# Delta heads' inverse from blocks of 16 instead of 8, half of the odd layer's lower halves on GpSimd, and odd-layer constants issued later

## The chip, the cores and the metric

The kernel runs on one core of a Trainium2 chip. The metric is the device time of one execution in microseconds (us). Three runs of the kernel before took 2287.2, 2292.83 and 2294.88 us, with a median of 2292.83. Engines are named as the profile names them: PE is the matrix engine (TensorE; PEld are its weight loads), DVE the vector engine, ACT the scalar engine, POOL is GpSimd, and SP is the queue that issues the DMA transfers.

## The reference

It is one inference step of two layers for a prompt of 1024 tokens and for 8 single samples, with the same weights; all data are fp32. Each layer normalizes x, projects it with one large matrix, runs its heads, gates them, and projects back:

```python
h = _rms(x, norm_w[layer]) * (1.0 + scale) + shift
# even layer: 8 gated-delta heads (A) and 8 mLSTM heads (B)
# odd layer:  4 GLA heads (C) and 4 retention heads (D)
y = jnp.concatenate([o_first, o_second], axis=-1) * jax.nn.silu(z)
x = x + gate * (y @ w_out)
```

A gated-delta head solves a unit lower triangular system in every chunk of tokens:

```python
kk = jnp.einsum('bthd,bshd->bhts', kc, kc)
A = jnp.where(tri_strict, decay * kk, 0.0) * beta_h[..., :, None]
U = lax.linalg.triangular_solve(A + eye, rhs, left_side=True, lower=True, unit_diagonal=True)
```

The outputs are the normalized x of prompt and samples and the new states of all heads.

## The kernel before

Prompt and samples stand side by side as 1032 columns (W), with the 1024 channels of x in 8 tiles of 128 partitions. Projections are computed in fp32 exactness from two halves: `load_w` (L889) loads a weight tile of 1024 rows by 128 columns in eight pieces (`wf`), and `halves` (L896) makes its rounded copy `whi` on ACT and the rest `wlo = wf - whi` on DVE. There are two buffers of each. Every projection then takes three matmuls per piece: whi with the high half of h, whi with the low half, and wlo with the high half. The columns are worked in three parts of 344 (NB), so a weight tile feeds 8 x 3 x 3 = 72 matmuls into three PSUM banks (`pj`).

All operations are recorded first (`Recorder`, L181) and not issued in the order of the code. A planner gives each a cost (`_cost` for DVE, ACT, POOL and SP; `_pe_cost`, L139, for PE), then places them on the five engines by readiness and priority (`forward`, L367), with priorities from a backward pass (`backward`, L310), several times over; the order with the shortest planned time is emitted. So each engine has a fixed order of instructions that depends on all the costs. An entry in `after` makes later recorded operations wait for a given one. As a consequence, nearly every row of the profile has one source line, L451, and rows are told apart by their tiles.

Gated-delta heads use chunks of 128 tokens, 8 chunks per head. `inverse` (L1293) gets the strictly lower triangular N of all chunks and forms the inverse of (I + N) by blocks. First, the 32x32 diagonal blocks (four per chunk) go to DRAM (`nd`), are read back so that each 8x8 diagonal block lies on a partition of its own (128 partitions), and DVE inverts these blocks by substitution, one column per step: 7 steps of two instructions. The result goes through DRAM again (`yd`) into the tile D (slot `EM`), 32 rows of four diagonal blocks side by side. Then the block size is doubled: 8 to 16 and 16 to 32 in the loop `for i in range(1, 3)`, each round with 32 matmuls of 32x32 (N times D), a masked copy on DVE, another 32 matmuls, a subtract and a 32x32 transpose on DVE; then 32 to 64 and 64 to 128 with larger matmuls. The identity that the substitution starts from is copied on POOL from the constant `i8`; the mask of each round is read out of the constant `icode`.

At the end of a layer, `out_proj` (L1947) reads the 16 tiles of y back from DRAM (`yd`) and splits each into halves (`split`). The tiles 14 and 15, which come last, are split late. `odd_setup` (L1660) loads the odd layer's constants: masks and decay tables (`lmask`, `rdm`, `rin`, `rend`), the low-rank weights (`gla_w2`), and the rotary tables. In the odd layer, POOL makes the products of the GLA heads (`s_tmp<-s_EM`), several of the rounding sums, and the `pow` of the norm.

Of the kernel before, what the change touches and what calls it, by code (L numbers as in the profile page):

```python
# [9 lines left out]
F32 = mybir.dt.float32  # L10
F32R = mybir.dt.float32r
AF = mybir.ActivationFunctionType
ALU = mybir.AluOpType
# [11 lines left out]
NC = T // L  # L25
# [14 lines left out]
def host_constants():  # L40
    f = np.float32
    c = {}
    c["ident"] = np.eye(128, dtype=f)
    pos = np.concatenate([np.arange(T), np.full(NS, 8192)]).astype(f)
    inv = (f(10000.0) ** (-np.arange(64, dtype=f) / f(64))).astype(f)
    ang = (pos[None, :] * inv[:, None]).astype(f).astype(np.float64)
    c["cosT"] = np.concatenate([np.cos(ang), np.cos(ang)], 0).astype(f)
    c["sinT"] = np.concatenate([np.sin(ang), -np.sin(ang)], 0).astype(f)
    lg = np.log(1.0 - 2.0 ** (-5.0 - np.arange(4)))
    s, t = np.arange(L)[:, None], np.arange(L)[None, :]  # L50
    dm = np.zeros((L, 4, L))
# [12 lines left out]

    code = np.zeros((32, 32), f)
    for i in range(2):
        code[lm[:, 1 - i, :].T > 0] = 1.0 + i
    c["icode"] = np.tile(code, (4, 1))
    c["i8"] = np.tile(np.eye(8, dtype=f).reshape(1, 64), (128, 1))

    sel = np.zeros((2, 4, 8, 4, 32), f)
    for to, at in enumerate((1, 0, 2, 3)):
        for i in range(8):
            sel[:, at, i, to, i] = 1.0
    c["sel"] = sel.reshape(64, 128)
    return c
# [62 lines left out]
def _pe_cost(method, out, args, kw):  # L139

    if method == "transpose":
        return (109.0 if args[1].shape[0] > 64 else 60.0), "whole"
    n, rows, cols = _elems(kw["rhs"]), kw["lhsT"].shape[0], kw["lhsT"].shape[1]
    if kw["rhs"].dtype == F32R:
        return 0.45 * n + 2.5, "pass"
    if kw.get("tile_position") is not None and cols <= 32:
        return (max(1.87 * n / 4, 15.0) if rows > 32 else 15.0), (rows, cols)
    if rows <= 64 and cols <= 64:
        return max(1.67 * n + 9, 117.0), (rows, cols)
    kind = "whole" if rows == 128 and (cols == 128 or kw.get("tile_position") is None) else (rows, cols)  # L150
    return 2 * max(0.833 * n + 2.5, 111.0) + 90 * (n == 130), kind
# [315 lines left out]
class Step:  # L467
# [428 lines left out]
    def halves(self, w, n=KT):  # L896
        hi, lo = (self.wtile(x, [128, KT, 128])[:, 0:n] for x in ("whi", "wlo"))
        self.act(hi, w[:, 0:n], AF.Copy)
        self.nc.vector.tensor_tensor(lo, w[:, 0:n], hi, op=ALU.subtract)
        return hi, lo  # L900

    def proj_parts(self, parts, ks):
# [390 lines left out]
    def inverse(self, N):  # L1293

        V, G, dma = self.nc.vector, self.nc.gpsimd, self.nc.sync.dma_start

        nd, yd = (self.nyd[x][self.turn(x, 2)] for x in ("nd", "yd"))
        by32 = lambda x, j: x.rearrange("(c j q) x -> c j (q x)", c=NC, j=4)[:, j, 0:1024].rearrange(
            "c (s t) -> s c t", t=32)
        by8 = lambda x: x[:, 0:256].rearrange("m (r t) -> m r t", t=32)[:, :, 0:8]  # L1300
        blocks = [slice(32 * j, 32 * j + 32) for j in range(4)]
        for j, b in enumerate(blocks):
            dma(by32(nd, j), N[b, :, b])
        n8, y8, t8 = (self.const([128, 8, 8], x) for x in ("n8", "y8", "t8"))
        dma(n8, by8(nd))
        G.tensor_copy(y8, self.i8)
        for s in range(7):
            n = 7 - s
            V.tensor_tensor(t8[:, 0:s + 1, 0:n], y8[:, 0:s + 1, s:s + 1].to_broadcast([128, s + 1, n]),
                            n8[:, s:s + 1, s + 1:8].to_broadcast([128, s + 1, n]), op=ALU.mult)  # L1310
            V.tensor_tensor(y8[:, 0:s + 1, s + 1:8], y8[:, 0:s + 1, s + 1:8], t8[:, 0:s + 1, 0:n], op=ALU.subtract)
        dma(by8(yd), y8)

        t = self.slot("EM", name="inv")
        D, At, qt, Dt = (t[:, 256 * i:256 * i + 256].rearrange("p (c t) -> p c t", c=NC) for i in range(4))
        for j, b in enumerate(blocks):
            dma(D[b], by32(yd, j))
        V.transpose(Dt, D)
        for i in range(1, 3):
            p = self.ps(None, [128, NC, 32])  # L1320
            for c in range(NC):
                for j, b in enumerate(blocks):
                    self.mm(p[b, c, :], N[b, c, b], Dt[b, c, :], tile_position=(32 * j, 32 * j))
            V.scalar_tensor_tensor(At, self.icode.unsqueeze(1).to_broadcast([128, NC, 32]), float(i), p,
                                   op0=ALU.is_equal, op1=ALU.mult)
            p = self.ps(None, [128, NC, 32])
            for c in range(NC):
                for j, b in enumerate(blocks):
                    self.mm(p[b, c, :], At[b, c, :], D[b, c, :], tile_position=(32 * j, 32 * j))
            V.tensor_tensor(D, D, p, op=ALU.subtract)  # L1330
            V.transpose(Dt, D)
        Y = self.slot("Y", [128, NC, L], name="Y")
        G.memset(Y, 0.0)
        for b in blocks:
# [12 lines left out]
        for c in range(NC):  # L1347
            for i in (0, 2):
                j = i + 1
# [271 lines left out]
    def even_setup(self):  # L1621
        nc, a, V, G = self.nc, self.a, self.nc.vector, self.nc.gpsimd
        self.bkq = self.const([128, 258], "bkq")
        G.memset(self.bkq, 0.0)
        self.icode = self.const([128, 16], "icode").bitcast(mybir.dt.bfloat16)
        self.i8 = self.c_load("i8", [128, 8, 8])
        zero = self.slot("aT", [128, 264], name="zero")
        G.memset(zero, 0.0)
        for x in self.nyd["yd"]:
            self.nc.sync.dma_start(x, zero)  # L1630
        code = self.slot("EM", [128, 32], name="code")
        self.nc.sync.dma_start(code, self.a["icode"])
        self.nc.vector.tensor_copy(self.icode, code)
        self.vs = self.const([128, 2, NS], "mvs")
        self.ozs = self.const([128, 2, NS], "mozs")
        self.nms = self.const([128, 2, 2, NS], "mnms")
        self.mC = self.const([128, 4, 130], "C")
        for x in range(2):
            G.memset(self.mC[64 - 64 * x:128 - 64 * x, 2 * x:2 * x + 2, :], 0.0)
        self.qq = self.const([128, 2, 2, NS], "mqq")  # L1640
        G.memset(self.qq, 0.0)

        nt = self.slot("q2", [32, 128], name="snt")
        nc.sync.dma_start(nt, a["state_mlstm_n"][0].rearrange("b (q x) d -> (b q) (x d)", x=2))
        p = self.ps()
# [13 lines left out]

    def odd_setup(self):  # L1660
        nc, a = self.nc, self.a
        self.lmask = self.c_load("lmask", [128, 6, 32])
        self.rdm = self.c_load("rdm", [128, 4, L])
        self.rin = self.c_load("rin", [128, 4, L])
# [5 lines left out]
        nc.sync.dma_start(self.cosT, a["cosT"])  # L1670
        self.sinT = self.slot("mk", name="sinT")
        nc.sync.dma_start(self.sinT, a["sinT"])
        self.glr = self.slot("va", name="glr")
        self.qk_w = [self.load_w(a["od_w_in"][0], c) for c in (0, 512)]

# [271 lines left out]
    def out_proj(self, src, l, mod):  # L1947
# [45 lines left out]
        def x_in(n):  # L1993
            x = xs[n % 2] if last else self.x_slot(n)
            nc.sync.dma_start(x, self.xd[l][n])
            return x
# [57 lines left out]
            G.tensor_tensor(wl[:, 1], w, wl[:, 0], op=ALU.subtract)  # L2054
        for k in late:
            split(k)
        x2 = [x_in(n) for n in range(2)]
        for n in range(2):
            for j in range(3):
# [61 lines left out]
    def build(self):  # L2121
        tc, nc = self.tc, self.nc
        with ExitStack() as ctx:
# [20 lines left out]
            self.sd = [dr.tile([16, 128], F32, name=f"sd{i}") for i in range(2)]  # L2144
            self.spd = dr.tile([16, W], F32, name="spd")
            self.rd = [dr.tile([4, QB], F32, name=f"rd{i}") for i in range(2)]
            self.nyd = {x: [dr.tile([128, 264], F32, name=f"{x}{i}") for i in range(2)] for x in ("nd", "yd")}
            self.program()
            with tc.manual_schedule():
                self.nc.emit()  # L2150
# [103 lines left out]
```

## Time and profile before

| | |
|---|---|
| Runs | 2287.2, 2292.83, 2294.88 us; median 2292.83 |
| Profiled execution | 2289.05 us, span 2287.0 us |
| PE busy | 2221.4 us (97%), 18844 instructions |
| DVE busy | 1382.8 us (60%), 2700 instructions |
| ACT busy | 747.7 us (33%), 1374 instructions |
| POOL busy | 527.7 us (23%), 385 instructions |
| Mean granted PE clock | 0.987 |

The first number of an engine is the time in which it had an instruction running, and the share is that of the span. The heads of the even layer lie from about 100 to 1175 us (the delta heads' inverses from 188 to 1085), the even layer's output projection from there to about 1360, and the odd layer from there to the end, with its output projection from about 2090 on. The place where the even layer's heads end and its output projection begins (1157 to 1180) is called the layer boundary. An fp32 matmul with fp32 operands is recorded twice, so a block of 32 small matmuls shows as 64 instructions. A matmul's duration is longer than its distance to the next one, since matmuls overlap; what it costs is read from the starts.

### The profile page before, as it was taken

The page shows a single profiled execution, that of the slowest core. Times are in us where ns is not written, and L with a number is a line of the kernel's source. Part 1 is how long each engine was busy: PE and PEld are TensorE (multiplying, and loading weights), DVE is VectorE, ACT ScalarE, POOL GpSimd, SP SyncE. Part 2 cuts the span into 40 slices and gives each one's busy share as a digit, 9 for nine tenths or more (in the row PEclk, how much of TensorE's full clock was granted, in tenths as well). Part 3 has the DMA queues.
Part 4 walks back from the last instruction along what each step waited for, and adds up shares of the span by engine and source line. Part 5 has one row for each costly group of instructions (what it writes and reads, how often), then busy time and mean ns, then how long its engine had stood idle before and what let it go on. Part 6 is the DMA issues. An engine that isn't in the chain of part 4 may idle for free.

```text
span 2287.0 us, 44726 instructions
## 1 busy us (share of the span) xinstructions
PE 2221.4 (97%) x18844; PEld 2070.0 (91%) x18844; DVE 1382.8 (60%) x2700; ACT 747.7 (33%) x1374; POOL 527.7 (23%) x385
## 2 busy tenths in 40 slices
PE   6999999999999999999989999999999999998998
PEld 5777788899999999899989999999999999997997
DVE  6774646565564646556453355876976876977332
ACT  4422323232233233232331134234225324334322
POOL 3121112111123012211330031422422422433100
PEclk8999999999999999999999999999999999998999
DMA  9362544422143212432362221233142143246222
GB/s 260 124 165 60 152 133 121 129 77 72 40 118 105 69 52 86 108 95 72 114 216 84 75 76 38 56 122 107 43 136 94 50 133 95 56 149 209 74 58 91
DMA packets 285455, 235.20 MB, mean 103 GB/s; under 512 B 47819, under 2 KB 257733, under 8 KB 285246
## 3 DMA queue, kind: packets, MB, share of 16 engines
q1 hardware_dynamic: 285254, 232.35, 34.6%
q8 instruction: 147, 2.41, 0.4%
q14 instruction: 54, 0.44, 0.1%
HBM read 185.59 MB, written 46.91 MB: 102 GB/s over the span
## 4 chain that ended last, share of the span: by engine, by line
PE 88%; DMA 4%; DVE 4%; issue 1%; ACT 1%; POOL 1%; SPq 1%; POOLq 0%; DVEq 0%; ACTq 0%
PE pj L451 68%; PE A L451 14%; PE B L451 6%; DMA wf<-in_ev_w_in 1%; SPq L451 1%; DMA s_aT<-rd 0%; DVE s_h L451 0%; DMA s_h<-in_x_prompt 0%; DVE arena L451 0%; DVE s_N L451 0%; DMA s_pt<-yd 0%; DVE s_pt L451 0%; DMA ed<-s_Y 0%; DMA s_mp<-gd 0%; DVE s_mp L451 0%
## 5 line engine op out<-in xcount | busy, mean ns | idle before, releaser
L451 PE MATMUL pj<-s_h,whi 128*128 128x344 f32 (+1 forms) x6024 | 1498.6, 327 | 10.8 <-ACT s_h L451 5.4
L451 PEld LDWEIGHTS pj<-s_h,whi 128*128 128x128 f32 (+1 forms) x6024 | 1042.7, 189 | 44.8 <-issue 25.3
L451 PE MATMUL pj<-s_h,wlo 128*128 128x344 f32 (+1 forms) x3024 | 982.2, 325 | 1.5 <-DVE wlo L451 0.9
L451 PEld LDWEIGHTS pj<-s_h,wlo 128*128 128x128 f32 (+1 forms) x3024 | 569.8, 189 | 16.1 <-issue 10.6
L451 DVE TENSOR_TENSOR wlo<-wf,whi 128x1024 fp32r<-128x1024 f32 (+1 forms) x144 | 192.9, 1340 | 291.2 <-ACT whi L451 272.3
L451 ACT ACTIVATE whi<-wf 128x1024 fp32r<-128x1024 f32 (+2 forms) x146 | 152.1, 1043 | 374.9 <-PE pj L451 330.3
L451 ACT ACTIVATE s_pt<-pj 128x344 f32<-128x344 f32 (+1 forms) x170 | 77.0, 453 | 288.3 <-PE pj L451 282.8
L451 POOL TENSOR_TENSOR arena<-arena,base 128x8 f32<-128x8 f32 (+5 forms) x38 | 64.4, 1697 | 377.8 <-DVE arena L451 377.1
L451 POOL TENSOR_TENSOR s_tmp<-s_EM 128x512 f32<-128x512 f32 (+1 forms) x60 | 88.5, 1493 | 156.2 <-PE A L451 69.1
L451 DVE SCALAR_TENSOR_TENSOR s_pt<-s_u,base,s_pt 128x1024 f32<-128x1024 f32 x72 | 96.5, 1341 | 0.3
L451 ACT ACTIVATE s_u<-pj 128x344 f32<-128x344 f32 x93 | 41.9, 453 | 142.4 <-PE pj L451 80.2
L451 DVE SCALAR_TENSOR_TENSOR arena<-arena,A 128x128 f32<-128x128 f32 (+1 forms) x84 | 32.8, 391 | 84.5 <-PE A L451 83.9
L451 DVE STREAM_TRANSPOSE s_kd<-s_u 32x256 f32<-32x256 f32 x128 | 55.8, 436 | 16.6 <-ACT s_u L451 13.5
L451 POOL TENSOR_TENSOR s_tmp<-s_tmp,arena 128x1024 f32<-128x1024 f32 (+2 forms) x26 | 43.4, 1676 | 88.6 <-PE A L451 62.2
L451 POOL TENSOR_TENSOR s_kd<-s_kd,s_vs 128x1032 f32<-128x1032 f32 x8 | 21.5, 2688 | 167.6 <-ACT s_vs L451 152.2
L451 DVE SCALAR_TENSOR_TENSOR s_zz<-s_pt,pj 128x344 f32<-128x344 f32 x96 | 48.4, 507 | 18.7 <-ACT s_pt L451 17.9
L451 DVE STREAM_TRANSPOSE s_vs<-s_v 32x256 f32<-32x256 f32 x128 | 55.8, 436 | 1.9
L451 ACT ACTIVATE arena<-A,arena 128x128 f32<-128x128 f32 x64 | 23.5, 368 | 100.8 <-PE A L451 100.5
L451 ACT ACTIVATE s_tmp<-s_tmp 128x1024 f32<-128x1024 f32 (+1 forms) x44 | 46.1, 1054 | 28.7 <-POOL s_tmp L451 24.0
L451 DVE SCALAR_TENSOR_TENSOR arena<-arena,B 64x130 f32<-64x130 f32 (+1 forms) x84 | 31.2, 371 | 38.6 <-PE B L451 37.2
L451 ACT ACT_TABLE_LOAD x41 | 52.6, 1283 | 5.2 <-DMA s_h<-in_x_prompt 4.5
L451 POOL MEMSET s_u<- 128x3 f32 x24 | 2.4, 101 | 208.5 <-DVE s_pt L451 208.5
(643 smaller groups left out, 3597.7 us busy)
## 6 DMA issues: line engine op xcount, KB each, us to landing
wf<-in_ev_w_in SPq DMA_DIRECT2D x64, 512.0 KB
wf<-in_od_w_in SPq DMA_DIRECT2D x48, 512.0 KB
wf<-in_ada_w SPq DMA_DIRECT2D x32, 512.0 KB
s_pt<-yd SPq DMA_DIRECT2D x24, 516.0 KB
s_tmp<-sd SPq DMA_DIRECT2D x24, 512.0 KB
yd<-s_qg SPq DMA_DIRECT2D x15, 516.0 KB
wf<-in_ev_w_out SPq DMA_DIRECT2D x14, 512.0 KB
wf<-in_od_w_out SPq DMA_DIRECT2D x14, 512.0 KB
```

The costliest lines, as they stand in the source:

```text
L451: op.fn(*[self.placed(x) for x in op.args], **{k: self.placed(x) for k, x in op.kw.items()})
```

## The change

It has four parts.

1. `inverse` starts from blocks of 16: 64 partitions hold one 16x16 block each, the substitution takes 15 steps of two DVE instructions, and one doubling (16 to 32) is left in front of the larger ones. The identity is loaded by DMA into the working tile, and the mask is a plain product with `imask`. `even_setup` loads imask and no longer builds icode and i8.
2. `_pe_cost` gives tiles of at most 32 columns a higher cost: 25.6 instead of 15 ns for 32 columns of data and more than 32 rows, and 18 instead of 15 ns for 32 rows or fewer.
3. `halves` puts every second subtract of the odd layer on POOL.
4. The loads of `odd_setup` up to the rotary tables are recorded with `after` set to the last split of out_proj.

```diff
     if kw.get("tile_position") is not None and cols <= 32:
-        return (max(1.87 * n / 4, 15.0) if rows > 32 else 15.0), (rows, cols)
+        return (max(0.8 * n, 20.0) if rows > 32 else 18.0), (rows, cols)
...
         self.act(hi, w[:, 0:n], AF.Copy)
-        self.nc.vector.tensor_tensor(lo, w[:, 0:n], hi, op=ALU.subtract)
+        (self.nc.gpsimd if self.layer == "odd" and self.turn("half", 2) else self.nc.vector).tensor_tensor(lo, w[:, 0:n], hi, op=ALU.subtract)
...
+        t = self.slot("EM", name="inv")
+        D, At, qt, Dt = (t[:, 256 * i:256 * i + 256].rearrange("p (c t) -> p c t", c=NC) for i in range(4))
+        nb, yb, tb = (t[0:64, 256 * i:256 * i + 256].rearrange("p (r t) -> p r t", t=16) for i in (1, 2, 3))
+        dma(yb, self.a["i16"].rearrange("p (r t) -> p r t", t=16))
         for j, b in enumerate(blocks):
             dma(by32(nd, j), N[b, :, b])
-        n8, y8, t8 = (self.const([128, 8, 8], x) for x in ("n8", "y8", "t8"))
-        dma(n8, by8(nd))
-        G.tensor_copy(y8, self.i8)
-        for s in range(7):
-            n = 7 - s
...
+        dma(nb, by16(nd))
+        for s in range(15):
+            n = 15 - s
+            V.tensor_tensor(tb[:, 0:s + 1, 0:n], yb[:, 0:s + 1, s:s + 1].to_broadcast([64, s + 1, n]),
+                            nb[:, s:s + 1, s + 1:16].to_broadcast([64, s + 1, n]), op=ALU.mult)
+            V.tensor_tensor(yb[:, 0:s + 1, s + 1:16], yb[:, 0:s + 1, s + 1:16], tb[:, 0:s + 1, 0:n], op=ALU.subtract)
+        dma(by16(yd), yb)
...
         V.transpose(Dt, D)
-        for i in range(1, 3):
-            p = self.ps(None, [128, NC, 32])
...
-            V.scalar_tensor_tensor(At, self.icode.unsqueeze(1).to_broadcast([128, NC, 32]), float(i), p,
-                                   op0=ALU.is_equal, op1=ALU.mult)
...
+        V.tensor_tensor(At, p, self.imask.unsqueeze(1).to_broadcast([128, NC, 32]), op=ALU.mult)
...
+        self.nc.after = (self.split_at,)
         self.lmask = self.c_load("lmask", [128, 6, 32])
         self.rdm = self.c_load("rdm", [128, 4, L])
         self.rin = self.c_load("rin", [128, 4, L])
...
         nc.sync.dma_start(self.sinT, a["sinT"])
+        self.nc.after = ()
...
         for k in late:
             split(k)
+        self.split_at = len(self.nc.ops) - 1
```

The order on each engine shows what moved. First PE, in one of the middle delta heads, before: `A<-s_EM,s_N` and `A<-s_EM` with 32x32 are the blocks of the doubling rounds, `pj` are projections and `B` is work of other heads.

```order
L451 MATMUL A_114<-s_EM_69,s_N_70 32x32 x32
L451 MATMUL B_117<-base,s_tmp_86 128x128
L451 MATMUL B_117<-arena,base 128x32
L451 MATMUL B_116<-base,arena 16x128
L451 MATMUL pj_112<-s_h_612,wlo_108 128x344
L451 MATMUL A_115<-s_EM_69 32x32 x32
...
L451 MATMUL A_113<-s_EM_69,s_N_70 32x32 x32
L451 MATMUL B_117<-arena,base 128x16
L451 MATMUL B_116<-s_va_75,s_mp_78 128x130
L451 MATMUL A_114<-s_EM_69 32x32 x32
```

The same place with the change:

```order
L448 MATMUL A_115<-s_EM_69,s_N_70 32x32 x32
L448 MATMUL B_116<-s_va_75,s_mp_78 128x130
L448 MATMUL B_116<-arena,s_qs_77 128x130
L448 MATMUL A_113<-s_EM_69 32x32 x32
L448 MATMUL B_117<-s_va_75,s_kwe_76 128x130
L448 MATMUL pj_111<-s_h_590,whi_106 128x344
...
L448 MATMUL B_116<-s_va_75,s_mp_78 128x130
L448 MATMUL A_114<-s_EM_69,s_N_70 32x32 x16
```

Of four blocks of 32 two are left ahead of the block of 16 that begins the next larger size.

Second the DMA queue SP at the boundary between the layers, before. The loads s_pt and s_u from yd are tiles of y for the output projection.

```order
L451 DMA out_p_mc<-arena 64x128
L451 DMA out_p_mn<-arena 64x1
L451 DMA arena<-in_rin 128x512
L451 DMA arena<-in_lmask 128x192
L451 DMA s_pt_83<-yd 128x1032
L451 DMA s_pt_84<-yd 128x1032
L451 DMA s_u_79<-yd 128x1032
L451 DMA s_pt_82<-yd 128x1032
L451 DMA wf_104<-in_ev_w_out 128x6x128
L451 DMA arena<-in_rdm 128x512
```

And with the change:

```order
L448 DMA out_p_mc<-arena 64x128
L448 DMA out_p_mn<-arena 64x1
L448 DMA s_pt_83<-yd 128x1032
L448 DMA s_pt_84<-yd 128x1032
...
L448 DMA s_zz_81<-xd 128x1032
L448 DMA arena<-in_gla_w 16x512 x2
L448 DMA arena<-in_lmask 128x192
L448 DMA s_pt_83<-xd 128x1032
L448 DMA arena<-in_rdm 128x512
L448 DMA arena<-in_rin 128x512
L448 DMA wf_105<-in_ev_w_out 128x2x128 x2
```

The constants now stand behind the last loads from yd and among those from xd, around the loads of the small weight tile.

Third POOL in the last retention head, before; s_kd, s_N, s_qg and s_h are sums of this head and of the output projection's input.

```order
L451 TENSOR_TENSOR s_kd_12573<-s_kd_12573,s_vs_12839 128x1032
L451 TENSOR_TENSOR s_q_18438<-s_pt_82,s_k_18427 128x1032
L451 TENSOR_TENSOR s_h_453<-s_pt_83,s_h_442 128x1032
L451 TENSOR_TENSOR s_N_12709<-s_N_12709,s_aT_12093 128x1032
L451 TENSOR_TENSOR s_qg_12653<-s_qg_12653,s_aT_12093 128x1032
L451 TENSOR_TENSOR s_qg_12653<-s_Y_12990,arena 128x1024
```

And with the change:

```order
L448 TENSOR_TENSOR s_kd_12163<-s_kd_12163,s_vs_12426 128x1032
L448 TENSOR_TENSOR wlo_108<-wf_104,whi_106 128x1024
L448 TENSOR_TENSOR s_q_18024<-s_pt_82,s_k_18011 128x1032
L448 TENSOR_TENSOR s_N_12300<-s_N_12300,s_aT_11683 128x1032
L448 TENSOR_TENSOR s_qg_12243<-s_qg_12243,s_aT_11683 128x1032
L448 TENSOR_TENSOR wlo_108<-wf_104,whi_106 128x768
L448 TENSOR_TENSOR s_h_454<-s_pt_83,s_h_443 128x1032
```

Two of the wlo subtracts have come in. At the start of the odd layer's block the same happens: one stands ahead of the two instructions `arena<-arena,base 128x2` and `88x1` (the norm's pow). In all 31 subtracts are on POOL, among them the last six before the final norm.

## Rows read from the trace of the kernel before

**Rows 1.** The page: busy time (share of the span) and instructions, and the chain.

```profile
PE 2221.4 (97%) x18844; PEld 2070.0 (91%) x18844; DVE 1382.8 (60%) x2700; ACT 747.7 (33%) x1374; POOL 527.7 (23%) x385
...
PE 88%; DMA 4%; DVE 4%; issue 1%; ACT 1%; POOL 1%; SPq 1%; POOLq 0%; DVEq 0%; ACTq 0%
```

**Rows 2.** Table by stretches: window, length, busy us (instructions) by engine, clock, DMA.

```profile
core 0: us, PE busy (x) PEld busy (x) DVE busy (x) ACT busy (x) POOL busy (x), PEclk, DMA share, GB/s
100.00:220.00 120.00, 108.02 (x1000) 94.05 (x999) 78.64 (x172) 31.97 (x75) 23.00 (x22) 0.97 0.44 114
220.00:700.00 480.00, 478.44 (x4400) 424.39 (x4399) 279.21 (x631) 141.16 (x272) 90.57 (x73) 1.00 0.37 105
2030.00:2090.00 60.00, 50.16 (x326) 45.43 (x325) 52.70 (x91) 27.02 (x37) 20.42 (x8) 0.89 0.65 212
```

**Rows 3.** Timeline of PE, one delta head: start, duration, instruction [idle before].

```profile
681.55 0.75 PE L451 MATMUL A<-s_EM,s_N 32*32 32x32 f32 x64 [0.16 <-DVE s_EM L451]
...
682.57 0.40 PE L451 MATMUL pj<-s_h,wlo 128*128 128x344 f32 x1
682.91 0.75 PE L451 MATMUL A<-s_EM 32*32 32x32 f32 x64
683.59 0.58 PE L451 MATMUL pj<-s_h,whi 128*128 128x344 f32 x2
684.01 0.32 PE L451 MATMUL pj<-s_h,wlo 128*128 128x344 f32 x1
684.17 0.47 PE L451 MATMUL pj<-s_h,whi 128*128 128x344 f32 x2
...
685.04 0.75 PE L451 MATMUL A<-s_EM,s_N 32*32 32x32 f32 x64
```

**Rows 4.** Groups of DVE's instructions by form: busy us, mean ns | idle before.

```profile
L451 DVE STREAM_TRANSPOSE s_EM<-s_EM 128x256 f32<-128x256 f32 x24 | 10.6, 442 | 7.1 <-DMA s_EM<-yd 6.6
...
L451 DVE TENSOR_TENSOR s_EM<-s_EM,A 128x256 f32<-128x256 f32 x16 | 6.7, 422 | 13.7 <-PE A L451 13.7
L451 DVE SCALAR_TENSOR_TENSOR s_EM<-arena,A 128x256 f32<-128x256 bf16 x16 | 6.7, 420 | 16.1 <-PE A L451 16.1
```

**Rows 5.** Timeline of DVE, the substitution of the same head.

```profile
671.34 2.66 DVE L451 TENSOR_TENSOR arena<-arena 128x7 f32<-128x7 f32 x13
```

**Rows 6.** Timeline of SP's DMA issues at the layer boundary.

```profile
1156.63 0.58 SPq L451 DMA_DIRECT2D arena<-in_rin  x1
1163.40 0.34 SPq L451 DMA_DIRECT2D arena<-in_lmask  x1
1163.83 0.85 SPq L451 DMA_DIRECT2D s_pt<-yd  x2
```

**Rows 7.** Timelines of DVE, ACT and PE at the layer boundary.

```profile
1159.24 1.23 DVE L451 TENSOR_TENSOR s_h<-s_pt,s_h 128x1032 fp32r<-128x1032 f32 x1 [3.17 <-ACT s_h L451]
...
1168.70 1.06 ACT L451 ACTIVATE s_h<-s_pt 128x1032 fp32r<-128x1032 f32 x1 [6.51 <-DMA s_pt<-yd]
...
1177.73 1.23 PE L451 MATMUL pj<-s_h,whi 128*128 128x344 f32 x3 [5.42 <-ACT s_h L451]
```

**Rows 8.** Timeline of PE, last retention head.

```profile
2061.34 0.43 PE L451 MATMUL pj<-s_mq,whi 128*128 128x344 f32 x1 [2.87 <-DVE s_mq L451]
...
2066.14 0.38 PE L451 MATMUL B<-base,s_u 128*8 128x128 f32 x1 [2.99 <-DVE s_aT L451]
```

**Rows 9.** Timelines of DVE and POOL, last retention head.

```profile
2044.60 2.82 DVE L451 TENSOR_TENSOR wlo<-wf,whi 128x1024 fp32r<-128x1024 f32 x1
...
2043.91 2.42 POOL L451 TENSOR_TENSOR s_q<-s_pt,s_k 128x1032 fp32r<-128x1032 f32 x1 [2.78 <-ACT s_k L451]
```

**Rows 10.** Timelines of POOL and PE at the start of the odd layer.

```profile
1355.63 1.86 POOL L451 TENSOR_TENSOR arena<-arena,base 128x2 f32<-128x2 f32 x2
...
1361.91 0.91 PE L451 MATMUL pj<-s_h,whi 128*128 128x344 f32 x2 [1.47 <-ACT s_q L451]
```

**Rows 11.** The page's costliest groups: instructions with wlo.

```profile
L451 PE MATMUL pj<-s_h,wlo 128*128 128x344 f32 (+1 forms) x3024 | 982.2, 325 | 1.5 <-DVE wlo L451 0.9
...
L451 DVE TENSOR_TENSOR wlo<-wf,whi 128x1024 fp32r<-128x1024 f32 (+1 forms) x144 | 192.9, 1340 | 291.2 <-ACT whi L451 272.3
```

More of the change, by code (lines that the diff above doesn't have):

```diff
@@ L63, in host_constants @@
     c["lmask"] = np.tile(lm, (4, 1, 1)).reshape(128, 192).copy()
[L65 to L69, printed above, removed]
+    c["imask"] = np.tile(lm[:, 0, :].T, (4, 1)).copy()
+    c["i16"] = np.tile(np.eye(16, dtype=f).reshape(1, 256), (64, 1))
     sel = np.zeros((2, 4, 8, 4, 32), f)
@@ L1299, in inverse @@
             "c (s t) -> s c t", t=32)
-        by8 = lambda x: x[:, 0:256].rearrange("m (r t) -> m r t", t=32)[:, :, 0:8]
+        by16 = lambda x: x[:, 0:512].rearrange("m (r t) -> m r t", t=32)[:, :, 0:16]
         blocks = [slice(32 * j, 32 * j + 32) for j in range(4)]
+        t = self.slot("EM", name="inv")
+        D, At, qt, Dt = (t[:, 256 * i:256 * i + 256].rearrange("p (c t) -> p c t", c=NC) for i in range(4))
+        nb, yb, tb = (t[0:64, 256 * i:256 * i + 256].rearrange("p (r t) -> p r t", t=16) for i in (1, 2, 3))
+        dma(yb, self.a["i16"].rearrange("p (r t) -> p r t", t=16))
         for j, b in enumerate(blocks):
             dma(by32(nd, j), N[b, :, b])
-        n8, y8, t8 = (self.const([128, 8, 8], x) for x in ("n8", "y8", "t8"))
-        dma(n8, by8(nd))
-        G.tensor_copy(y8, self.i8)
-        for s in range(7):
-            n = 7 - s
[L1309 to L1315, printed above, removed]
+        dma(nb, by16(nd))
[5 more added lines that the diff above has]
+        dma(by16(yd), yb)
         for j, b in enumerate(blocks):
@@ L1318, in inverse @@
         V.transpose(Dt, D)
-        for i in range(1, 3):
-            p = self.ps(None, [128, NC, 32])
-            for c in range(NC):
-                for j, b in enumerate(blocks):
-                    self.mm(p[b, c, :], N[b, c, b], Dt[b, c, :], tile_position=(32 * j, 32 * j))
-            V.scalar_tensor_tensor(At, self.icode.unsqueeze(1).to_broadcast([128, NC, 32]), float(i), p,
-                                   op0=ALU.is_equal, op1=ALU.mult)
[L1326 to L1331, printed above, removed]
+        p = self.ps(None, [128, NC, 32])
+        for c in range(NC):
+            for j, b in enumerate(blocks):
+                self.mm(p[b, c, :], N[b, c, b], Dt[b, c, :], tile_position=(32 * j, 32 * j))
+        V.tensor_tensor(At, p, self.imask.unsqueeze(1).to_broadcast([128, NC, 32]), op=ALU.mult)
+        p = self.ps(None, [128, NC, 32])
+        for c in range(NC):
+            for j, b in enumerate(blocks):
+                self.mm(p[b, c, :], At[b, c, :], D[b, c, :], tile_position=(32 * j, 32 * j))
+        V.tensor_tensor(D, D, p, op=ALU.subtract)
+        V.transpose(Dt, D)
         Y = self.slot("Y", [128, NC, L], name="Y")
@@ L1624, in even_setup @@
         G.memset(self.bkq, 0.0)
-        self.icode = self.const([128, 16], "icode").bitcast(mybir.dt.bfloat16)
-        self.i8 = self.c_load("i8", [128, 8, 8])
+        self.imask = self.const([128, 32], "imask")
+        self.nc.sync.dma_start(self.imask, self.a["imask"])
         zero = self.slot("aT", [128, 264], name="zero")
@@ L1629, in even_setup @@
         for x in self.nyd["yd"]:
[L1630 to L1633, printed above, removed]
+            self.nc.sync.dma_start(x.rearrange("m (a b) -> (m a) b", a=2), zero)
         self.vs = self.const([128, 2, NS], "mvs")
@@ L2146, in build @@
             self.rd = [dr.tile([4, QB], F32, name=f"rd{i}") for i in range(2)]
-            self.nyd = {x: [dr.tile([128, 264], F32, name=f"{x}{i}") for i in range(2)] for x in ("nd", "yd")}
+            self.nyd = {x: [dr.tile([64, 528], F32, name=f"{x}{i}") for i in range(2)] for x in ("nd", "yd")}
             self.program()
```

## The prediction

> **What bounds the kernel now.** First the busy table and the chain of waits of the page: TensorE (PE) is busy 2221.4 of 2287.0 us, and 88% of the chain that ended last is PE [rows 1]. A kernel like this gets faster in two ways only: PE is given less to do, or one of its few idle stretches closes. So the second view is the table by stretches [rows 2]. From 220 to 700 us, where the delta heads run, PE is busy 478.44 of 480 us while VectorE (DVE) is busy 279.21: everything DVE, ScalarE (ACT) and GpSimd (POOL) do there lies beside PE work. PE idles at the start (12.0 of the 120 us from 100 to 220) and in the last retention head (9.8 of the 60 us from 2030 to 2090). Two more gaps show in the timeline: 5.42 us at the layer boundary [rows 7] and 1.47 us at the start of the odd layer [rows 10]. The third view, the timeline of single stretches, prices the edits.
>
> **Inverse, PE.** The order of PE shows four blocks of 32 small matmuls per head before and two after. In the trace such a block is one row x64 [rows 3]. What it displaces: the block at 682.91 starts 0.68 us before the next matmul (683.59). That is the lower end, with nothing for the change of shape. From the projection matmul ahead (682.57) to 683.59 it is 1.02 us; a projection matmul alone takes 0.16 us (684.01 to 684.17), so the block with its switch takes 0.86 us, the upper end. Some blocks stand between other small matmuls and switch cheaper, so I take the middle, 0.78 us. Two blocks of 8 heads: 16 x 0.78 = 12.5 us (10.9 to 13.8). PE has work queued on either side, so this goes off the end one for one, provided the fill lasts; that proviso is the first rival.
>
> **Inverse, DVE and latency.** Removed per head: one transpose, one product with a mask, one subtract, 0.442 + 0.420 + 0.422 = 1.28 us [rows 4]. Added: 30 substitution instructions for 14. Of the old ones 13 took 2.66 us, 0.205 each [rows 5], at a mean of 12 elements per partition (84 elements in 7 steps). The new ones have 680 elements in 15 steps, a mean of 45. From 0.205 us at 12 to 0.422 at 256 elements is 0.9 ns per element, so 0.03 us more: 30 x 0.235 = 7.05 us against 14 x 0.205 = 2.87, or +4.2. Net DVE +2.9 us per head, 23 us over the heads, in stretches where DVE has over 40% free [rows 2]. Latency: +4.2 us of substitution, less the vanished round from 681.55 to 685.04, 3.49 us [rows 3]: +0.7 us on a chain that ran beside full PE. I cost it at nothing. What hides it is the projections of the next head; if they ran out, 8 x 0.7 = 6 us would show, and with 4.2 us per head unhidden 34 us. The matrix still goes through DRAM in as many pieces (each twice as long), and an identity load takes the place of a POOL copy: beside PE work as well, nothing.
>
> **Constants issued later.** On SP the loads of rin and lmask stood ahead of four loads from yd that feed the last group of the even layer's output projection. rin went out at 1156.63; lmask, queued behind it, only at 1163.40, for its region was still being read by two output transfers; the yd load came at 1163.83 [rows 6]. So the queue stood for 6.2 us (from 1157.21). ACT then waited 6.51 us for that yd load, and PE 5.42 us for ACT [rows 7]. After the change the yd loads come right behind the output transfers. The buffer of the first load was read until 1160.47 by a DVE sum (1159.24 and 1.23 us, [rows 7]), so at most 3.4 us of the 6.2 fall away; at least nothing, if the other buffers come free later. I take 2 us, nearer to the row. What is late next: the constants themselves, five of them now around the first loads of the next weights, one issue of 0.34 to 0.58 us each [rows 6], some 2 us of SP; PE has no gap there now, and it may cost 1 us. It is inside the 2.
>
> **Halves on POOL.** 31 of the odd layer's subtracts go from DVE to POOL. On DVE the group is 144 instructions of 1340 ns mean, and PE waited for them 0.9 us in the whole kernel [rows 11]: moving them can win nothing where PE is full. On POOL a sum of this size took 2.42 us [rows 9]: 31 x 2.42 = 75 us there, 31 x 1.34 = 42 us off DVE. DVE matters in one place, the last retention head, where PE waits 2.87 us for s_mq and 2.99 us for s_aT, both from DVE [rows 8]. Ahead of those stand the subtract at 2044.60 and others; after the change two of the head's subtracts are on POOL. Bounds: a win of 5.9 us (both waits), or a loss of 2.4 us, when one POOL subtract delays a sum that feeds the same head; the second of the two stands where that could be. That one is behind s_N and s_qg, two sums that wait for a DMA, and is itself not wanted before the head ends. DVE is freed of at least 1.34 us; I take a win of 2.
> What bears against it: the subtract at 2044.60 took 2.82 us while POOL ran from 2043.91 to 2046.33, over twice its mean of 1.34 [rows 9, 11]. The Trainium skill ("SBUF — State Buffer", section on the two separate sides) says that VectorE and GpSimd share one port pair as an exclusive lock: a VectorE instruction with two SBUF inputs and a GpSimd one that reads SBUF block each other fully. The trace agrees in these rows. By that rule the 31 moves would free DVE of no time at all wherever a two-input instruction is next (75 us held against 42 freed), and the 2 us here would be a loss of about 1. The sum keeps the 2, because most of DVE's work in that head is transposes and PSUM reads.
>
> **Start of the odd layer.** On POOL a subtract of 2.42 us now stands ahead of the two power instructions, 1.86 us together at 1355.63, that gate the norm [rows 10]; PE already had a 1.47 us gap behind them at 1361.91. Cost 0 (PE's order puts more projection work there) to 2.4 us; I take 1, as the matmuls of the norm's second third come earlier in the new order.
>
> **New PE costs in the plan.** They change no instruction, only the order, everywhere. The lows are at the start, 12.0 us of idle between 100 and 220: it may gain or lose a few. Nothing in the trace prices this; 0, with 5 us either way in the range.
>
> **Sum.** -12.5 - 2 - 2 + 1 = -15.5 us. The profiled execution took 2289.05 us: 2273.6. It ran 3.8 us under the median of 2292.83, so against the runs shown 2277.
>
> **The rivals.**
> 1. *Given back.* The shorter inverse leaves PE at the same points waiting for the same chains (weights from DMA, the conv and the norm on DVE), so the 12.5 us of work turn into 12.5 us of idle. For it: DVE gains 23 us in the same stretch. Against it: PE idles 1.6 of 480 us there, that is, it is the work that sets the pace. Time: 2292.8 - 4 + 1, about 2290.
> 2. *More than the sum.* The boundary at its upper end (3.4), both waits of the last head gone (5.9), nothing lost at the odd layer's start: 2292.8 - 12.5 - 3.4 - 5.9 = 2271. For it: both gaps are ends of one DVE or SP queue that the change shortens. Against it: in the last head each wait that goes is followed by one on the next sum of the same full DVE queue.
> 3. *Slower: POOL's subtracts come late.* A weight tile feeds 72 projection matmuls of 0.16 us, 11.3 us. POOL runs in order; where a POOL queue behind a DMA wait or behind s_tmp products is longer than that, PE stops at the first matmul with wlo. Two buffers of wlo stand between, so it decides once a subtract is over 11 us behind its hi copy. If each of the 31 then costs its extra 2.42 - 1.34 = 1.1 us, that is +34 us: 2292.8 - 12.5 - 2 + 34 = 2312; a third of them gives 2290. For it: POOL was held by DVE and DMA waits in the last head. Against it: one tile in two only, and 0.9 us of wlo wait now.
> 4. *The reordered plan loses* 10 us or more at the start or the boundary while the rest comes true: 2287 or above.
> That the change doesn't do what it says is excluded for the blocks, since the new order holds 16 fewer of them; for the boundary it is rival 1.
>
> **Chances.** A measurement of this kernel tells about 0.3%, 6.9 us, from no change: faster is under 2286, slower over 2299.7. Forecast 0.50 (2270 to 2284), more than the sum 0.17, given back 0.18 (a quarter of it still under 2286), POOL late 0.10 (0.07 over 2299.7), reordered plan 0.05 (0.03 over 2299.7, 0.02 within). Faster: 0.50 + 0.17 + 0.05 = 0.72. Slower 0.10. Within: 0.18. The range from 2264 to 2291 takes in the second rival, with 5 us more for the unpriced plan, 1.3 for the inverse at its upper end and 1 for rounding, and the given-back case; it leaves out the slower ones and some 0.06 below.
>
> **What would show it.** PE's busy time down by 11 to 14 us with 1024 fewer of its instructions, the same idle from 220 to 1140; the substitution at 6.5 to 7.5 us; yd loads out by 1161 (on the old clock) and the boundary gap 3 us or so; PE's wait for wlo under 3 us in all; waits for s_mq and s_aT shorter by about 2 us. The forecast is wrong if PE's busy time falls and its idle rises by as much (rival 1), or if "PE pj waits for POOL wlo" is among the first rows of PE's waits (rival 3).

## The result and the profile after

The changed kernel took 2273.89 us (median of 4 runs, 2269.0 to 2275.8) against 2290.86 us before (4 runs): ratio 0.9922, 95% interval [0.9898, 0.9947], 17 us faster. Predicted were 2277 us, from a sum of -15.5. The total came out; several of its terms did not, as the experiments show.

The page of the changed kernel, its busy times and chain, against [rows 1]:

```profile
PE 2206.5 (97%) x17820; PEld 2056.0 (90%) x17820; DVE 1379.6 (61%) x2771; ACT 745.8 (33%) x1374; POOL 604.7 (27%) x409
...
PE 87%; DVE 5%; DMA 5%; issue 1%; SPq 1%; ACT 1%; POOL 0%; POOLq 0%; DVEq 0%; ACTq 0%
```

PE has 1024 instructions fewer and 14.9 us less to do. The span fell by 13.3 us (2287.0 to 2273.7 us in the two profiled executions; that of the changed kernel is its slowest of four), so PE idles 1.6 us more in all. Where it idles has changed. The table by stretches of the changed kernel, columns as in [rows 2]:

```profile
100.00:220.00 120.00, 108.29 (x864) 92.20 (x864) 73.53 (x182) 31.08 (x73) 23.37 (x21) 0.94 0.47 118
220.00:700.00 480.00, 474.70 (x3894) 421.64 (x3893) 287.06 (x682) 141.36 (x275) 89.88 (x69) 1.00 0.38 105
...
2020.00:2080.00 60.00, 51.81 (x345) 49.11 (x344) 53.47 (x91) 28.02 (x37) 25.47 (x10) 0.91 0.64 217
```

From 220 to 700 us PE idles 5.3 us instead of 1.6 [rows 2]. The last retention head (now 10 us earlier) idles 8.2 instead of 9.8 us.

The substitution is one group of DVE in the page of the changed kernel (busy, mean ns of one):

```profile
L448 DVE TENSOR_TENSOR s_EM<-s_EM 64x15 f32<-64x15 f32 (+7 forms) x240 | 49.2, 205 | 13.5 <-DMA s_EM<-nd 7.7
```

30 instructions per head take 49.2 / 8 = 6.15 us; predicted were 7.05 from [rows 5].

At the layer boundary, the issues of SP in the changed kernel:

```profile
1152.53 0.86 SPq L448 DMA_DIRECT2D out_p_mn<-arena  x1
1157.89 2.60 SPq L448 DMA_DIRECT2D s_pt<-yd  x2
...
1178.28 0.37 SPq L448 DMA_DIRECT2D arena<-in_lmask  x1
```

and its ACT and PE there, against [rows 7]:

```profile
1164.31 1.06 ACT L448 ACTIVATE s_h<-s_pt 128x1032 fp32r<-128x1032 f32 x1 [4.74 <-DMA s_pt<-yd]
...
1173.35 0.75 PE L448 MATMUL pj<-s_h,whi 128*128 128x344 f32 x3 [3.66 <-ACT s_h L448]
```

The yd load goes out 5.9 us earlier than in [rows 6]. PE reaches the gap 2.6 us earlier than before (1169.69 against 1172.31) and leaves it 4.4 us earlier. SP still stands 4.5 us in front of the load (1153.39 to 1157.89), now for the buffer it writes, which a DVE sum reads until 1157.86; this is the bound that the prediction set. The gap of PE shrinks from 5.42 to 3.66 us.

The waits of PE in the last retention head of the changed kernel, against [rows 8]:

```profile
2050.51 0.42 PE L448 MATMUL pj<-s_mq,whi 128*128 128x344 f32 x1 [1.39 <-DVE s_mq L448]
2052.47 1.07 PE L448 MATMUL B<-s_tmp,arena 128*32 128x256 f32 x16 [0.75 <-DVE s_aT L448]
2057.14 1.23 PE L448 MATMUL pj<-s_mk,whi 128*128 128x344 f32 x3 [3.60 <-ACT s_mk L448]
2060.82 0.65 PE L448 MATMUL pj<-s_va,whi 128*128 128x344 f32 x1 [2.46 <-DVE s_va L448]
```

The waits for s_mq and s_aT fell from 5.86 to 2.14 us, and 6.06 us of others (s_mk, s_va) stand right behind: of the two old ones little is gained.

### The profile page after: what moved, and what is told of

The parts are those of the page before. It is cut to its first block, busy times and chain, and to the rows that moved or that the text cites. A ratio compares the mean times of both kernels' runs of the same rounds, so it can differ in the third digit from the quotient of the medians.

```text
span 2273.7 us, 42794 instructions
## 1 busy us (share of the span) xinstructions
PE 2206.5 (97%) x17820; PEld 2056.0 (90%) x17820; DVE 1379.6 (61%) x2771; ACT 745.8 (33%) x1374; POOL 604.7 (27%) x409
## 4 chain that ended last, share of the span: by engine, by line
PE 87%; DVE 5%; DMA 5%; issue 1%; SPq 1%; ACT 1%; POOL 0%; POOLq 0%; DVEq 0%; ACTq 0%
PE pj L448 68%; PE A L448 14%; PE B L448 5%; SPq L448 1%; DMA wf<-in_ev_w_in 1%; DMA wf<-in_ada_w 1%; DMA yd<-s_EM 1%; DVE wlo L448 1%; DMA s_h<-in_x_prompt 1%; DVE s_EM L448 0%; DVE arena L448 0%; DVE s_N L448 0%; DVE s_tmp L448 0%; DMA s_EM<-yd 0%; DVE s_zz L448 0%
## 5 line engine op out<-in xcount | busy, mean ns | idle before, releaser
L448 DVE TENSOR_TENSOR wlo<-wf,whi 128x1024 fp32r<-128x1024 f32 x112 | 145.7, 1301 | 259.3 <-ACT whi L448 235.9
L448 ACT ACTIVATE whi<-wf 128x1024 fp32r<-128x1024 f32 (+1 forms) x146 | 152.3, 1043 | 380.3 <-PE pj L448 308.9
L448 POOL TENSOR_TENSOR wlo<-wf,whi 128x1024 fp32r<-128x1024 f32 (+1 forms) x32 | 79.9, 2497 | 179.8 <-ACT whi L448 179.8
L448 POOL TENSOR_TENSOR s_kd<-s_kd,s_vs 128x1032 f32<-128x1032 f32 x8 | 19.3, 2411 | 160.0 <-ACT s_vs L448 142.8
L448 DVE TENSOR_TENSOR s_EM<-s_EM 64x15 f32<-64x15 f32 (+7 forms) x240 | 49.2, 205 | 13.5 <-DMA s_EM<-nd 7.7
```

Source lines behind the costliest of these rows:

```text
L448: op.fn(*[self.placed(x) for x in op.args], **{k: self.placed(x) for k, x in op.kw.items()})
```

## The experiments

Twelve kernels ran, in four groups. Each ratio is against runs of the kernel before in the same group; 0.001 is 2.3 us. Words such as "the kernel of 6" mean the kernel of that experiment. In most of the expectations theory W says that the PE work removed is the gain; theory R, its rival, that the new order of the plan is.

**1. The new inverse alone.** The kernel before with the first part of the change (all edits in `inverse`, its constants and `even_setup`):

```diff
-        for s in range(7):
+        for s in range(15):
...
-        for i in range(1, 3):
-            p = self.ps(None, [128, NC, 32])
+        p = self.ps(None, [128, NC, 32])
```

> The kernel before with the new inverse alone (blocks of 16; plan costs, halves and constants as before). Theory W (the PE work that goes is the gain): 12.5 us less PE work, little of it given back, so 9 to 13 us faster than before, ratio 0.994 to 0.996, and 1024 PE instructions fewer with 12 to 15 us less PE busy time. Theory R (the new order is the gain): the longer substitution and its trip through DRAM reopen idle time in the delta heads, so 3 to 7 us faster, ratio 0.997 to 0.999, and the rest of the 17 us comes from the other three parts.

Measured: 2272.38 against 2287.09 us, ratio 0.9926 [0.9913, 0.9940]. The inverse alone makes the whole 17 us, more than the 9 to 13 of W and far from R. Its page:

```profile
PE 2196.7 (97%) x17820; PEld 2052.5 (91%) x17820; DVE 1405.8 (62%) x2803; ACT 746.4 (33%) x1374; POOL 528.6 (23%) x377
```

PE busy is down by 24.7 us, at nearly the same granted clock (0.988 against 0.987). Its idle rose, by 2.7 us over the span. (The profiled execution is the fastest of the five; its span is 22.0 us shorter, where the medians differ by 15 and the ratio gives 17.) The largest new gap is one that the sum did not have. ACT and PE of this kernel, in the recurrence of the first delta head:

```profile
222.37 1.06 ACT L448 ACTIVATE whi<-wf 128x1024 fp32r<-128x1024 f32 x1 [7.64 <-DMA wf<-in_ev_w_in]
223.33 0.44 ACT L448 ACTIVATE s_u<-pj 128x344 f32<-128x344 f32 x1
223.67 0.36 ACT L448 ACTIVATE arena<-A,arena 128x128 f32<-128x128 f32 x1
...
224.08 0.80 PE L448 MATMUL A<-arena,s_kd 128*128 128x128 f32 x2 [6.33 <-ACT arena L448]
```

The row to read is the first: the cast of a weight tile stands at the head of ACT's queue and waits 7.64 us for its DMA. Two steps behind it stands the small product that the head's recurrence waits for, and so PE waits 6.33 us for 0.36 us of ACT work. The same gap stands in the kernels of 6 and 10 below (6.11 and 6.52 us). It is absent from the changed kernel and from the kernel of 7, which have the new inverse too: it comes with the order of the plan and not with the longer substitution as such.

**2. The new PE costs alone.**

```diff
-        return (max(1.87 * n / 4, 15.0) if rows > 32 else 15.0), (rows, cols)
+        return (max(0.8 * n, 20.0) if rows > 32 else 18.0), (rows, cols)
```

> The kernel before with the new PE cost line alone: the same instructions in another order. Theory W: within 3 us of before, ratio 0.9987 to 1.0013. Theory R: 4 to 8 us faster, ratio 0.9965 to 0.998, seen as shorter PE idle at 1869 us and in the last retention head and as fewer changes between tile shapes.

Measured: ratio 1.0012 [0.9996, 1.0028]. Within W, though the interval reaches beyond it; R is out for this part.

**3. Every second lower half of the odd layer on GpSimd alone.**

```diff
-        self.nc.vector.tensor_tensor(lo, w[:, 0:n], hi, op=ALU.subtract)
+        (self.nc.gpsimd if self.layer == "odd" and self.turn("half", 2) else self.nc.vector).tensor_tensor(lo, w[:, 0:n], hi, op=ALU.subtract)
```

> The kernel before with every second lower half of the odd layer on GpSimd alone. Theory W: 0 to 3 us faster, all of it in the last retention head (PE idle there 9.8 us before), ratio 0.9987 to 1.000. Theory R: 3 to 6 us faster, because the plan of the whole odd layer gets shorter. Theory P (the shared port eats it): 0 to 4 us slower.

Measured: ratio 1.0006 [0.9997, 1.0016]: no change that the runs can tell. It lies just outside W, within P, and R is out. In the place where W expected the gain, PE lost. The stretch from 2010 to 2110 us, the kernel before and then this one:

```profile
2010.00:2110.00 100.00, 90.16 (x678) 83.13 (x677) 78.22 (x129) 42.32 (x60) 34.47 (x16) 0.93 0.59 190
```

```profile
2010.00:2110.00 100.00, 86.10 (x580) 79.19 (x573) 72.00 (x123) 42.81 (x60) 35.90 (x16) 0.90 0.54 179
```

DVE's busy time there falls by 6.2 us and PE idles 4.1 us more. The wait of PE for s_aT is now the longest of the head (the table of PE's waits of this kernel, us in total, times, longest):

```profile
PE B L451 <- DVE s_aT L451: 7.7, 1, 7.7
```

It is made by DVE, whose queue puts sixteen transposes in front of it. These are DVE's rows, and PE's row behind them:

```profile
2053.12 7.18 DVE L451 STREAM_TRANSPOSE s_vs<-s_v 32x256 f32<-32x256 f32 x16
2060.33 0.69 DVE L451 TENSOR_TENSOR s_aT<-B,arena 128x512 f32<-128x512 f32 x1
...
2061.08 0.38 PE L451 MATMUL B<-base,s_u 128*8 128x128 f32 x1 [7.72 <-DVE s_aT L451]
```

In the kernel before, the same sum came later:

```profile
2065.39 1.29 DVE L451 TENSOR_TENSOR s_aT<-B,arena 128x512 f32<-128x512 f32 x2
```

So the sum did come forward, by 5.1 us (2065.39 to 2060.33). But in this plan PE asks for it 9.8 us earlier, before the products with s_mq and not behind them: it stops at 2053.36, where it stopped at 2063.15 before ([rows 8], 2066.14 less 2.99).

DVE in the whole kernel fell from 1382.8 to 1352.4 us, by 30.4, where 32 subtracts of 1.34 us would be 42.9. So some 12 us came back as longer DVE instructions. What makes them longer shows in one product of two SBUF tiles with 8 columns, which in this kernel starts beside a subtract on POOL. First this kernel, then the kernel before:

```profile
1389.36 2.40 POOL L451 TENSOR_TENSOR wlo<-wf,whi 128x1024 fp32r<-128x1024 f32 x1 [14.68 <-ACT whi L451]
1389.60 2.17 DVE L451 TENSOR_TENSOR arena<-s_q,s_k 128x8 f32<-128x8 f32 x1 [5.21 <-ACT s_k L451]
```

```profile
1393.03 0.16 DVE L451 TENSOR_TENSOR arena<-s_q,s_k 128x8 f32<-128x8 f32 x1
```

It takes 2.17 us in place of 0.16 and ends as POOL's subtract ends (1391.77 and 1391.76). The other three products of this kind took 2.11 to 2.18 us. The Trainium skill ("SBUF — State Buffer", section on the two separate sides) has the two engines lock each other out of one port pair for a whole instruction. These rows agree; over the kernel the price is about a quarter of the time that was moved.

**4. The constants later, alone.**

```diff
+        self.nc.after = (self.split_at,)
```

> The kernel before with the odd layer's constants issued later alone. Theory W: 1 to 3 us faster, from the gap of 5.4 us at the layer boundary, ratio 0.9987 to 0.9996. Theory R: no gain in itself (within 1 us), as the gap is then ended by the next late buffer.

Measured: ratio 0.9988 [0.9978, 0.9998], 2.7 us faster. The gap at the boundary went from 5.42 to 2.79 us. As W had it.

**5. The first doubling left out of the kernel before, with nothing in its place.**

```diff
-        for i in range(1, 3):
+        for i in range(2, 3):
```

> The kernel before with its first doubling round (8 to 16) left out and nothing in its place, so that the inverse is not complete: the same 16 blocks of matmuls go, and no substitution gets longer. If the longer substitution is fully hidden (theory W), this is as fast as the new inverse alone, ratio 0.991 to 0.994. If it costs what its latency adds (30 instructions for 14, 4 us per head), this is 6 to 30 us faster than the new inverse alone, ratio under 0.990.

Measured: ratio 0.9835 [0.9818, 0.9853], 2252.36 against 2287.62 us, and by the ratios about 20 us faster than the new inverse alone. By the expectation this would make the substitution the culprit. The stretch of the delta heads, from 185 to 1140 us, in the kernel before, with the new inverse alone, and with the round left out:

```profile
185.00:1140.00 955.00, 948.28 (x8878) 867.18 (x8877) 542.13 (x1240) 291.05 (x594) 192.54 (x153) 1.00 0.33 93
```

```profile
185.00:1140.00 955.00, 937.59 (x7912) 862.42 (x7911) 575.15 (x1341) 291.14 (x599) 201.64 (x148) 0.99 0.35 98
```

```profile
185.00:1140.00 955.00, 948.88 (x8000) 875.52 (x7999) 561.54 (x1245) 298.88 (x624) 206.51 (x157) 1.00 0.36 98
```

PE idles 6.7, 17.4 and 6.1 us. So 11 us of the 20 lie here, and 6.3 of these are the gap shown under 1. At the boundary the new inverse alone waits 9.0 us (7.58 and 1.42), and with the round left out 1.1 us. These two places make the difference, which is 16.0 us in the spans of the two profiled executions; PE's busy time is alike (2196.7 and 2197.5 us). The idle in the heads can be the substitution's latency or the plan's order; experiment 7 makes the substitution longer.

**6. Inverse and constants**, without new costs and halves: the edits of 1 and 4.

> The new inverse and the later constants, without the new PE costs and without halves on GpSimd. If the parts add (-17 and -2.7 us): ratio 0.990 to 0.993, 1 to 4 us faster than the changed kernel, with a boundary gap of 3 to 5 us in place of the 9.0 us (7.6 and 1.4) of the new inverse alone. If what the planner makes of each input is chance of a few us, it lies anywhere from 0.991 to 0.995.

Measured: 2258.15 against 2287.62 us, ratio 0.9861 [0.9843, 0.9878], 32 us faster than before and about 16 faster than the changed kernel, so the best complete kernel here, and outside both ranges that were expected. The parts do not add: -17 and -2.7 gave -32. The boundary gap is down to 1.1 us (0.19 and 0.93), and the page says

```profile
PE 2194.3 (97%) x17820; PEld 2050.8 (91%) x17820; DVE 1402.6 (62%) x2803; ACT 747.3 (33%) x1374; POOL 529.3 (23%) x377
```

at a granted clock of 0.991 (0.988 with the inverse alone). Against the profiled execution of 1 the span is 11.0 us shorter: 8.6 us of this is less idle, nearly all of it at the boundary, and 2.4 us is less busy time. In the heads PE still idles 16.9 us.

**7. Each product of the substitution computed twice**, in the kernel of 6.

```diff
             V.tensor_tensor(tb[:, 0:s + 1, 0:n], yb[:, 0:s + 1, s:s + 1].to_broadcast([64, s + 1, n]),
                             nb[:, s:s + 1, s + 1:16].to_broadcast([64, s + 1, n]), op=ALU.mult)
+            V.tensor_tensor(tb[:, 0:s + 1, 0:n], yb[:, 0:s + 1, s:s + 1].to_broadcast([64, s + 1, n]),
+                            nb[:, s:s + 1, s + 1:16].to_broadcast([64, s + 1, n]), op=ALU.mult)
```

> Inverse and constants alone (2258 us), with each product of the substitution computed twice: 15 instructions of 0.2 us more per head, the same result. If the substitution shows in the PE's idle of the delta heads (theory S: 16.5 us there against 5.6 us with the round left out and no longer substitution), the 3 us per head show too: 8 to 25 us slower, ratio 0.990 to 0.997, with 25 us of idle or more in the heads. If it is hidden and the idle there comes from the plan (theory H), within 3 us, ratio 0.985 to 0.988.

Measured: ratio 0.9919 [0.9903, 0.9935], 13 us slower than 6 by the ratios, at a lower granted clock (0.986 against 0.991). The time is that of theory S. But in the heads PE idles 19.3 us (16.9 in kernel 6):

```profile
185.00:1140.00 955.00, 935.71 (x7877) 856.02 (x7875) 591.17 (x1437) 291.08 (x591) 198.25 (x148) 0.99 0.34 96
```

The group of the substitution grew from 47.5 to 74.1 us, and 2.4 us of idle came there, so on balance most of the added latency is covered, as the prediction said of the 4.2 us it priced. But the 2.4 is a balance. The gap of 6.11 us behind the late cast is gone in this plan, and others have opened: waits for the DMA of in_ada_w (6.0 us in all), and in one head this one, at the end of the substitution's chain:

```profile
564.14 1.08 PE L448 MATMUL A<-s_EM,s_N 32*32 32x32 f32 x64 [5.41 <-DVE s_EM L448]
```

PE waits there for the transpose behind the substitution, which in turn had waited 9.05 us for the substitution's result to come back from DRAM; kernel 6 waits 1.06 us at this place. So cover is not sure in every head, and whether the longer chain or its place in this plan made this gap was not separated. The rest of the 13 us is elsewhere in the new plan.

**8. The other three parts together**, with the old inverse.

> The changed kernel with the old inverse: the other three parts together. Theory W, from the three single runs (+2.7, +1.4 and -2.7 us): within 3 us of before, ratio 0.9987 to 1.0013. Theory R (the parts help each other): 4 to 8 us faster, ratio 0.9965 to 0.998.

Measured: ratio 0.9979 [0.9964, 0.9994], 5 us faster. Between W and R; the single runs (+2.7, +1.4, -2.7) sum to 1.4.

**9. The changed kernel again**, unchanged, on the chip that ran 5, 6 and 8.

> The changed kernel again, for a comparison on one chip. Theory W: the ratio of the new inverse alone with the three small parts on top, 0.9915 to 0.994. Theory R: clearly under it, 0.990 or less.

Measured: ratio 0.9933 [0.9916, 0.9951], as in the result.

**10 and 11. The changed kernel without the new costs, and without the halves on GpSimd** (the edits of 2 and of 3 undone).

> The changed kernel with the old PE costs: inverse, constants and halves on GpSimd. Theory K (the new PE cost line gives back what the inverse won): as fast as inverse and constants alone, ratio 0.985 to 0.988. Theory G (the halves on GpSimd give it back): as slow as the changed kernel, ratio 0.991 to 0.995. Theory C (any other plan loses or wins some us by chance): in between.

> The changed kernel with all halves on VectorE: inverse, constants and the new PE costs. Theory K: as slow as the changed kernel, ratio 0.991 to 0.995. Theory G: as fast as inverse and constants alone, ratio 0.985 to 0.988. Theory C: in between.

Measured: ratios 0.9941 [0.9924, 0.9957] and 0.9946 [0.9930, 0.9962]. Neither K nor G as they stood: either of the two parts, put on top of 6, takes it back to the time of the changed kernel, and both together cost no more than one. In the trace they do it in different places. With the halves (10) the last retention head: PE is busy 87.55 of 100 us from 2010 to 2110 against 93.98 in kernel 6, which is shown first:

```profile
2010.00:2110.00 100.00, 93.98 (x622) 88.38 (x621) 72.66 (x118) 46.74 (x71) 35.55 (x14) 0.97 0.53 172
```

```profile
2010.00:2110.00 100.00, 87.55 (x546) 81.88 (x546) 70.47 (x103) 43.42 (x56) 43.98 (x18) 0.90 0.51 166
```

Of the 6.4 us more idle, some 3.4 stand behind the head, in waits for s_tmp at the start of the output projection (1.94 and 2.28 us, where kernel 6 waits 0.78). The granted clock of the whole run falls from 0.991 to 0.987. With the costs (11) it is the boundary: gaps of 3.62 and 1.90 us where 6 has 0.19 and 0.93. And PE is busy 2210.0 us over the span, 15.7 more than in 6, with the same instructions. The largest part of this that a group shows is that of the 128 matmuls with the weights in_ada_w (shift, scale and gate), in 6 and in 11:

```profile
L448 PE MATMUL pj<-wf,base 128*32 128x512 f32 x128 | 34.4, 617 | 2.7 <-DMA wf<-in_ada_w 2.7
```

```profile
L448 PE MATMUL pj<-wf,base 128*32 128x512 f32 x128 | 42.0, 633 | 3.5 <-DMA wf<-in_ada_w 3.5
```

**12. Kernel 6 with a touch on one planned cost**: the same instructions in another order.

```diff
-        return 0.45 * n + 2.5, "pass"
+        return 0.45 * n + 2.6, "pass"
```

> Inverse and constants alone (ratio 0.986), with the planned cost of a projection matmul at 0.45 n + 2.6 ns instead of 2.5: the same instructions, another plan by no more than a touch. If the halves and the new PE costs each give back their own 15 us or so (theories K and G together), this stays at 0.985 to 0.988. If a new plan by itself moves the time by as much (theory C), it can lie anywhere up to 0.994, with PE idle in other places than inverse and constants alone had.

Measured: 2263.1 us, ratio 0.9889 [0.9867, 0.9912]; 6 us slower than 6 by the ratios, with intervals that overlap a little. So this one new plan by itself moved the time by some 6 us. Kernel 6 may be a lucky plan by that much; the intervals of 10 and 11 lie clear of this one, with about 12 us between. That the halves and the costs as such take these 12 us back is not shown. One new plan does not bound what others do: in experiment 7 the plan lost 13 us, 2.4 of them in the heads. And on top of the other part each of the two costs nothing (9 against 10 and 11). Theory C stands beside K and G.

What the twelve do show together is where the gain comes from. The complete kernels with the new inverse (1, 6, 7 and 9 to 12) all lie between 0.9861 and 0.9946, and those with the old one (2, 3, 4 and 8) between 0.9979 and 1.0012, whatever else was changed and however the plan fell (5, whose inverse is not complete, is left aside).

## Why the prediction was right, and where it was not

- *Inverse, PE (-12.5)*. The mechanism is right: PE has less to do, and little of it came back as idle (rival 1 did not come). The term was too small. The inverse alone brought 17 us; in its profiled execution PE's busy time fell by 24.7 us and its idle rose by 2.7. In the changed kernel busy time fell by 14.9 us, just over the 11 to 14 that the prediction named. The blocks themselves account for 13.1 of the 24.7. Their two groups (busy us, mean ns of one) in the kernel before:

```profile
L451 PE MATMUL A<-s_EM 32*32 32x32 f32 x1408 | 19.9, 194 | 0.1
L451 PE MATMUL A<-s_EM,s_N 32*32 32x32 f32 x1280 | 18.4, 194 | 3.0 <-issue 1.9 <-DVE s_EM L451 1.0
```

and with the inverse alone:

```profile
L448 PE MATMUL A<-s_EM 32*32 32x32 f32 x896 | 13.3, 193 | 1.1 <-DVE s_EM L448 1.1
L448 PE MATMUL A<-s_EM,s_N 32*32 32x32 f32 x768 | 11.9, 193 | 2.3 <-DVE arena L448 1.4 <-DVE s_EM L448 0.9
```

38.3 and 25.2 us. The price of a block from [rows 3] was thus good (16 x 0.78 = 12.5). The remaining 11.6 us of busy time are spread over other groups of the same instructions in another order (the 128 matmuls `pj<-wf,base` alone went from 37.0 to 33.6 us); which step of the plan gives them is open.
- *Inverse, DVE and latency (0)*. Supported on balance: the substitution took 6.15 us per head, and computing its products twice (26.6 us more in all) brought 2.4 us more idle in the heads, with one gap of 5.41 us on its own chain. The cover was not complete in the changed kernel either: "the same idle from 220 to 1140" is wrong, it rose from 4.0 to 9.4 us. In the kernels of 1 and 6 the largest gap that was located (6.33 and 6.11 us) is not the substitution but the late weight cast on ACT.
- *Constants later (-2)*. Right: 2.7 us alone; in the changed kernel the gap fell by 1.8 us (5.42 to 3.66), and the next one grew by 0.5 (1.42 to 1.91).
- *Halves on POOL (-2)*. Wrong. By the trace 32 subtracts went to POOL, not 31. In time the part is +1.4 us alone, with an interval that holds zero. In three pairs that differ in this alone PE idles more from 2010 to 2110 us with them: 4.1 us more on the kernel before (90.16 to 86.10), 6.4 on kernel 6 (93.98 to 87.55), and 2.3 on the kernel of 11 (94.08 to 91.81, the latter the changed kernel). The step that failed is that a DVE freed of two subtracts shortens PE's waits for its sums: in experiment 3 s_aT came 5.1 us earlier, but the new plan had PE ask for it 9.8 us earlier, and the wait rose from 2.99 to 7.72 us. In the changed kernel other waits (s_mk, s_va) took the place of the two old ones. What bore against the term, DVE being held while POOL works, came true in single rows (0.16 to 2.17 us); over the odd layer it took back about 12 of the 42.9 us moved, not all of them. Rival 3, PE waiting for wlo, did not come: 0.3 us in the changed kernel, 0.9 before.
- *Start of the odd layer (+1)*. Wrong: POOL does its subtract ahead of the pow (1351.80, 2.39 us), and yet the gap of 1.47 us is gone: PE idles 0.4 us in all from 1340 to 1400. The prediction's lower bound of 0, PE's order putting more projection work there, was the one to take.
- *New PE costs (0, 5 either way)*. Within its range alone (+2.7 us). Between kernels 6 and 11, which differ in this alone, 19 us were lost by the ratios, far outside the 5: 5.2 us of idle, and 15.7 us of longer busy time of the same instructions, about 11 of it beyond what the clock can explain. On top of 10 the same line costs nothing, so the loss belongs to the pair of plans.

So -15.5 was near the measured -17 because an inverse that is worth more than its term stood beside parts that were worth less than theirs. That the direction and the mechanism came out is merit; that the total came out this close is luck. The measured time is also near rival 2's 2271 us, but not by its road: the boundary gained 1.8 us and not 3.4, and the last head 1.6 us and not 5.9.

## What to carry to other kernels

Where one engine is busy 97% of the span, the work taken off it is the part of a change to price first, and a single-part run of it is the first experiment. In a kernel whose order a planner sets, price a part that only reorders at zero with a range of the plan's own scatter (here 6 us in the one try that changed nothing else, and possibly more), and measure parts in combination: the best complete kernel had two of the four parts, and with either or both of two that cost nothing alone it was 16 to 19 us slower. Moving work off a busy engine does not shorten the waits for its results where the new order asks for them earlier still.

## What was not expected of the hardware

The same PE instructions took 15.7 us more in another order (2194.3 and 2210.0 us in kernels 6 and 11), of which the lower granted clock over the span explains about 5 by estimate (0.991 and 0.989 of some 2250 us). A product of 8 columns on VectorE took 2.17 us in place of 0.16 when it started beside a subtract on GpSimd. An instruction of ACT of 0.36 us held PE for 6.33 us, for the 7.64 us that a cast of weights ahead of it waited for a transfer.
